# Softmax tiles turned by VectorE and a trip through DRAM in place of TensorE transposes

## The chip, the cores and the metric

The kernel runs on one core of one Trainium2 chip. A core has a matrix engine (TensorE, PE in the profile, with its weight loads shown as PEld), a vector engine (VectorE, DVE), an activation engine (ScalarE, ACT), a general engine (GpSimd, POOL) and a queue engine (SyncE, SP), all working in order, each on its own list of instructions; sixteen DMA engines move data between DRAM and the on-chip memory (SBUF). TensorE writes its results to PSUM, which the profile names ps with a tag. The metric is the device time of one execution in microseconds (us); lower is better.

## The reference

One layer of an encoder over 512 tokens of width 1024, all in float32:

- four token mixers fed by one input projection of h = RMSNorm(x): A, a differential attention with 4 heads (two softmaxes per head, subtracted, over chunks of 64 tokens); F, a forgetting attention with 8 heads of 64 (causal, with a bias from a cumulative sum); C, a convolution of width 31 with a LayerNorm; D, a short gated convolution. Each is projected to 1024, gated by sigmoids of h, summed, and projected again;
- a cross attention into 256 memory tokens;
- a gated MLP of width 2816 with a convolution of width 3.

The change lies in A and F. For a block of 128 queries:

```python
# A, per head: two softmaxes, subtracted, applied to v
p = softmax(where(mask, q @ k.T * scale, -inf))      # for c = 0 and 1
a = p[0] - lam * p[1]
o = a @ v
# F, per head
s = q @ k.T * scale + c_q - c_k
p = softmax(where(t_k <= t_q, s, -inf))
o = p @ v
```

## The kernel before

**Number format.** Products with float32 accuracy are made from three matmuls: each operand is split into a high part (a cast by ACT to the fp32r format) and a low part (the remainder, by DVE), and high x high, high x low and low x high are summed. Weights arrive in the raw tile `wr` by DMAs that SP issues (L175), ACT casts them to `wh` (L189), DVE makes `wl` (L190). There are four `wh` and four `wl` buffers, and weights are prepared three blocks ahead of the matmuls that use them. A block of the main work is 24 matmuls of 512 columns.

**Main work and background tasks.** The main line of the program is a sequence of such blocks (projections, gates, branch projections). The attentions are Python generators beside it, `a_task` (one per head) and `f_task` (one per pair of heads). An object `Background` counts a clock from the matmuls that the program has issued (`bg.clock`); a task's step ends with `yield cost, wait`, and it is taken up again when `wait` us of that clock have gone by and credit for `cost` is there. At most two tasks are open at a time, and `bg.drain` issues what is left of a task at once. Behind this, a planner orders the instructions of each engine by a priority from the program order and by its own estimate of when each becomes ready; on the chip each engine then follows its list in order.

**An attention task.** Queries come in four tiles of 128, keys up to the tile's end, so tile qt has (qt + 1) x 128 keys. In step s = 0 to 3 the scores of query tile s are made (PE, into PSUM tag `sc`), DVE takes the row maximum (L829 in A, L994 in F, where the bias tile `fbias`, made by POOL in L988 and L990, is added), ACT takes the exponential with its row sum (L834, L999), and DVE or ACT scales by the reciprocal (L838 and L839 in A, L1003 in F). The result lies in tile `e` as queries x keys. For the product with v it is needed as keys x queries. So in step s + 1, `to_keys_major` turns the tile of step s: TensorE transposes each 128 x 128 part into PSUM tag `tr` (L235), ACT casts it to `pth` (L154), and DVE makes `ptl` (L155). In steps 3 and 5 `values` multiplies two query tiles at a time: step 3 query tiles 0 and 1, step 5 query tiles 2 and 3. It issues matmuls of 256 columns, and of 128 for the last key tile. A's heads have three passes per key tile, F's two, since F's v holds its high and low part side by side in one stationary operand.

**Order and buffers around it.** A's four tasks run beside the last gate blocks of mixer C, F's four pairs beside those of mixer A. F's pair p + 1 does not pass its step 1 before pair p has finished. `e` has 3 buffers, `fbias` 2, `pth` and `ptl` 2 each; the PSUM tags `mm`, `av`, `sc` and `tr` have 2 banks each, and while the attentions run the main work uses only `mm`. After the last pair of F comes its own branch projection, whose matmuls need F's result `y`, with two gate blocks before them.

Of the kernel before, what the change touches and what calls it, by code (L numbers as in the profile page):

```python
# [16 lines left out]
F32 = mybir.dt.float32  # L17
F32R = mybir.dt.float32r
# [64 lines left out]
def hybrid_layer(ctx: ExitStack, tc: tile.TileContext, a: dict, out: bass.AP):  # L83
# [150 lines left out]
    def transpose(ps, x, n=P):  # L234
        PE.transpose(ps, x, ident[:n, :n])  # L235
        bg.clock += 0.107
# [544 lines left out]
        matmul(ps[:, :w], qk[:, c, q], qk[:, 2 + c, :w], True, False)  # L781
        matmul(ps[:, :w], qk[:, c, q], qk[:, 4 + c, :w], False, True)

    def to_keys_major(e, n, pt_h, pt_l, local):

        ps = bank("tr")
        for kt in range(n):
            transpose(ps[:, kt * P:(kt + 1) * P], e[:, kt * P:(kt + 1) * P])
        sl = slice(local * P, (local + 1) * P)
        split(ps[:, :n * P].rearrange("p (k c) -> p k c", k=n), pt_h[:, :n, sl], pt_l[:, :n, sl])  # L790

    def values(ps, terms, pt, half):


        n = 2 * half + 2
        for kt in range(n):
            q0 = P if kt == n - 1 else 0
            passes = terms(kt)
            for i, (v, p) in enumerate(passes):
                matmul(ps[:, half * 256 + q0:half * 256 + 256], v, pt[p][:, kt, q0:256],  # L800
                       kt == 0 and i == 0, kt == n - 1 and i == len(passes) - 1)

    def pt_tiles():
        return (m1p.tile([P, 4, 256], F32R, tag="pth", name="pth", bufs=2),
                m1p.tile([P, 4, 256], F32R, tag="ptl", name="ptl", bufs=2))


    def a_task(h, qk, v):
        es, pt, av = {}, None, None
        for step in range(6):  # L810
            if step in (3, 5):
                if av is None:
                    av = bank("av")
                vh, vl = (x[:, :, h * P:(h + 1) * P] for x in v[0])
                values(av, lambda kt: ((vh[:, kt], 0), (vh[:, kt], 1), (vl[:, kt], 0)), pt, step // 2 - 1)
            cost = 0.0
            if 1 <= step <= 4:
                if step in (1, 3):
                    pt = pt_tiles()
                to_keys_major(es.pop(step - 1)[:, 0], step, pt[0], pt[1], (step - 1) % 2)  # L820
                cost += 0.1 + 0.15 * step
            if step < 4:
                qt, w = step, (step + 1) * P
                e = es[qt] = e4()
                st = m1p.tile([P, 8], F32, tag="st8", name="st8", bufs=4)
                for c in range(2):
                    ps = bank("sc")
                    scores(ps, qk, c, qt * P, w)
                    V.tensor_tensor_reduce(e[:, c, :w], ps[:, :w], mask_a[:, S - w:], scale=1.0,  # L829
                                           scalar=-3.0e38, op0=ALU.add, op1=ALU.max,  # L830
                                           accum_out=st[:, c:c + 1])
                V.tensor_scalar(st[:, 2:4], st[:, 0:2], -HD ** -0.5, None, ALU.mult)
                for c in range(2):
                    A.activation(e[:, c, :w], e[:, c, :w], AF.Exp, bias=st[:, 2 + c:3 + c],  # L834
                                 scale=HD ** -0.5, accum_out=st[:, 4 + c:5 + c])
                V.reciprocal(st[:, 6:8], st[:, 4:6])
                V.tensor_scalar(st[:, 7:8], st[:, 7:8], lam, None, ALU.mult)
                A.activation(e[:, 1, :w], e[:, 1, :w], AF.Copy, scale=st[:, 7:8])  # L838
                V.scalar_tensor_tensor(e[:, 0, :w], e[:, 0, :w], st[:, 6:7], e[:, 1, :w], ALU.mult,  # L839
                                       ALU.subtract)  # L840
                cost += 0.6 + 0.0035 * w
            if step == 5:
                e = e4()
                A.copy(e[:, 0], av)
            yield cost, 3.5

        ps = bank("tr")
        for t in range(NT):
# [102 lines left out]
    def f_task(p, qk, v):  # L951
        f_steps[p] = 0
        while f_steps[p - 1] < 4:
            yield 0.0, 0.5
        ck = []
        for j in range(2):
            t = m1p.tile([P, S], F32, tag="ck", name="ck", bufs=2)
            G.dma_start(t, crows[2 * p + j:2 * p + j + 1, :].rearrange("a s -> (a s)").partition_broadcast(P))
            ck.append(t)
        yield 0.0, 2.0  # L960
        es, pts, av = {}, None, None
        for step in range(6):
            if step in (3, 5):
                if av is None:
                    av = [bank("av"), bank("av")]
                for j in range(2):
                    hl = v[0][:, :, 2 * p + j]
                    values(av[j], lambda kt: ((hl[:, kt], 0), (hl[:, kt], 1)), pts[j], step // 2 - 1)
            while step == 1 and f_steps[p - 1] < 6:
                yield 0.0, 0.5  # L970
            f_steps[p] = step + 1
            cost = 0.0
            if 1 <= step <= 4:
                if step in (1, 3):
                    pts = [pt_tiles() for _ in range(2)]
                e = es.pop(step - 1)
                for j in range(2):
                    to_keys_major(e[:, j], step, pts[j][0], pts[j][1], (step - 1) % 2)
                cost += 0.1 + 0.3 * step
            if step < 4:  # L980
                qt, w = step, (step + 1) * P
                e = es[qt] = e4()
                st = m1p.tile([P, 8], F32, tag="st8", name="st8", bufs=4)
                for j in range(2):
                    head = 2 * p + j
                    bias = m1p.tile([P, S], F32, tag="fbias", name="fbias", bufs=2)

                    G.tensor_scalar(bias[:, :w], ck[j][:, :w], -1.0, cq[:, qt, head:head + 1],  # L988
                                    ALU.mult, ALU.add)
                    G.affine_select(out=bias[:, w - P:w], in_=bias[:, w - P:w], pattern=[[-1, P]],  # L990
                                    compare_op=ALU.is_ge, fill=BIG, base=0, channel_multiplier=1)
                    ps = bank("sc")
                    scores(ps, qk, j, qt * P, w)
                    V.tensor_tensor_reduce(e[:, j, :w], ps[:, :w], bias[:, :w], scale=1.0,  # L994
                                           scalar=-3.0e38, op0=ALU.add, op1=ALU.max,
                                           accum_out=st[:, j:j + 1])
                V.tensor_scalar(st[:, 2:4], st[:, 0:2], -HD ** -0.5, None, ALU.mult)
                for j in range(2):
                    A.activation(e[:, j, :w], e[:, j, :w], AF.Exp, bias=st[:, 2 + j:3 + j],  # L999
                                 scale=HD ** -0.5, accum_out=st[:, 4 + j:5 + j])  # L1000
                V.reciprocal(st[:, 6:8], st[:, 4:6])
                for j in range(2):
                    V.tensor_scalar(e[:, j, :w], e[:, j, :w], st[:, 6 + j:7 + j], None, ALU.mult)  # L1003
                cost += 0.6 + 0.0038 * w
            yield cost, 4.5
        if "f" not in y:
            y["f"] = (y8(), y8())

        e = e4()
        for j in range(2):  # L1010
            A.copy(e[0:HD, j], av[j][HD:P])
            V.tensor_tensor(e[j * HD:(j + 1) * HD, 0], av[j][0:HD], e[0:HD, j], ALU.add)
        split(e[:, 0], y["f"][0][:, p], y["f"][1][:, p])
        yield 1.8, 0.0
# [717 lines left out]
```

## Time and profile before

| what | value |
|---|---|
| time, median of 3 runs | 1063.66 us (1062.95 to 1064.75) |
| time of the profiled execution | 1062.93 us |
| span of its instructions | 1060.7 us |
| TensorE busy | 1050.7 us, 5357 matmuls |
| DVE, ACT, POOL busy | 796.7, 497.1, 148.1 us |
| A's attention lies at about | 230 to 365 us of the span |
| F's attention lies at about | 390 to 530 us of the span |

How to read it: a line of a group is `line engine operation out<-in shapes xcount | busy us, mean ns of one | idle time of the engine before them, and what ended it`. A line in order of time begins with its start and its length in us; neighbours of one kind are merged (x4), and in brackets stands how long the engine had been idle and who released it. A matmul's own length is that of one instruction in a pipeline, so the distance between the starts of two tells more than the length of one. The profile does not count issuing a DMA as busy time. `ACTq`, `SPq` and `POOLq` are the engines' queues of such issues.

### The profile page before, as it was taken

To read this page: it belongs to the slowest core of one execution; us is meant where nothing else is said; L and a number is where in the kernel's file an instruction comes from. 1 tells how busy PE (TensorE), PEld (TensorE's weight loads), DVE (VectorE), ACT (ScalarE), POOL (GpSimd) and SP (SyncE) were. 2 spreads that over 40 slices of the span, in tenths; PEclk is the share of its full clock that TensorE was granted. 3 is DMA by queue.
4 is the path that set the end of the run, shared out by engine and by line. 5 is a ranking of instruction groups with operands and counts; after the bars stand their busy time and mean duration, and the time that the engine had idled before them with its cause. 6 is when DMAs were issued, how large, how long until landed. Compare 5 with 4: busy or idle time off the path is not lost.

```text
span 1060.7 us, 14540 instructions
## 1 busy us (share of the span) xinstructions
PE 1050.7 (99%) x5357; PEld 892.6 (84%) x5357; DVE 796.7 (75%) x1261; ACT 497.1 (47%) x817; POOL 148.1 (14%) x248
## 2 busy tenths in 40 slices
PE   9999999999999999999999999999999999999997
PEld 7888888888888988888888899999888888888885
DVE  6999997567666358766575888786778787777796
ACT  5322222367565256655443665664333333445662
POOL 4000000000001015322110031031111211111001
PEclk9999999999999999999999999999999999999999
DMA  8944333322222252332344744226566776725672
GB/s 278 300 144 104 107 93 99 96 84 80 78 81 62 54 147 88 94 98 81 120 140 144 267 144 119 81 80 198 179 224 213 237 228 211 236 80 179 206 220 80
DMA packets 162107, 152.57 MB, mean 144 GB/s; under 512 B 5567, under 2 KB 135212, under 8 KB 162037
## 3 DMA queue, kind: packets, MB, share of 16 engines
q1 hardware_dynamic: 153139, 120.04, 37.6%
q10 hardware_dynamic: 6338, 23.08, 5.8%
q0 software_dynamic: 2560, 8.54, 2.8%
q8 instruction: 42, 0.69, 0.3%
q14 instruction: 28, 0.23, 0.1%
HBM read 133.79 MB, written 17.84 MB: 143 GB/s over the span
## 4 chain that ended last, share of the span: by engine, by line
PE 94%; DMA 2%; DVE 2%; ACT 1%; issue 1%; SPq 0%; POOLq 0%; DVEq 0%; POOL 0%; ACTq 0%
PE ps_mm L231 51%; PE ps_av L231 29%; PE ps_sc L231 6%; PE ps_tr L235 3%; PE ps_tr L231 2%; DMA dw<-sums 2%; DVE wl L1534 1%; PE ps_mm L440 1%; DMA e<-in_w_in 1%; PE ps_av L440 1%; ACT wh L1533 0%; DVE o L1632 0%; DVE htl L1534 0%; DVE n L1534 0%; ACT n L1533 0%
## 5 line engine op out<-in xcount | busy, mean ns | idle before, releaser
L189 ACT CAST wh<-wr 128x1024 fp32r<-128x1024 f32 (+1 forms) x142 | 148.6, 1050 | 273.6 <-PE ps_mm L231 173.5
L190 DVE TENSOR_TENSOR wl<-wr,wh 128x1024 fp32r<-128x1024 f32 (+1 forms) x142 | 178.0, 1256 | 89.4 <-ACT wh L189 89.1
L231 PE MATMUL ps_mm<-hth,wh 128*128 128x512 f32 (+1 forms) x616 | 231.4, 382 | 0.3 <-ACT hth L154 0.2
L231 PE MATMUL ps_mm<-htl,wh 128*128 128x512 f32 (+1 forms) x616 | 230.1, 380 | 0.0
L231 PE MATMUL ps_mm<-hth,wl 128*128 128x512 f32 (+1 forms) x616 | 229.8, 379 | 0.0
L231 PEld LDWEIGHTS ps_mm<-hth,wh 128*128 128x128 f32 x616 | 114.1, 188 | 21.7 <-ACT hth L154 0.8
L231 PEld LDWEIGHTS ps_mm<-hth,wl 128*128 128x128 f32 x616 | 114.0, 188 | 21.0
L231 PEld LDWEIGHTS ps_mm<-htl,wh 128*128 128x128 f32 x616 | 114.1, 188 | 20.4
L231 PE MATMUL ps_av<-hth,wh 128*128 128x512 f32 (+1 forms) x328 | 122.6, 374 | 0.0
L231 PE MATMUL ps_av<-htl,wh 128*128 128x512 f32 (+1 forms) x328 | 122.5, 373 | 0.0
L231 PE MATMUL ps_av<-hth,wl 128*128 128x512 f32 (+1 forms) x328 | 122.4, 373 | 0.0
L662 DVE SCALAR_TENSOR_TENSOR y<-y,par,y 128x482 f32<-128x482 f32 (+29 forms) x120 | 83.6, 738 | 0.2
L231 PEld LDWEIGHTS ps_av<-hth,wl 128*128 128x128 f32 x328 | 61.6, 188 | 10.8
L231 PEld LDWEIGHTS ps_av<-hth,wh 128*128 128x128 f32 x328 | 61.6, 188 | 10.8
L231 PEld LDWEIGHTS ps_av<-htl,wh 128*128 128x128 f32 x328 | 61.6, 188 | 10.8
L1534 DVE TENSOR_TENSOR wl<-dw,wh 128x1024 fp32r<-128x1024 f32 x32 | 40.2, 1261 | 12.8 <-ACT wh L1533 12.6
L1533 ACT CAST wh<-dw 128x1024 fp32r<-128x1024 f32 x32 | 33.5, 1051 | 22.6 <-PE ps_tr L231 7.5
L988 POOL TENSOR_SCALAR fbias<-ck,cq 128x128 f32<-128x128 f32 (+3 forms) x32 | 27.5, 865 | 68.8 <-DVE st L994 63.5
L1482 ACT ACTIVATE th<-c 128x512 f32<-128x512 f32 x22 | 13.9, 631 | 48.6 <-DVE c L592 45.9
L154 ACT CAST pth<-ps_tr 128x512 fp32r<-128x512 f32 (+3 forms) x56 | 23.4, 448 | 22.1 <-PE ps_tr L235 21.9
L592 DVE SCALAR_TENSOR_TENSOR c<-ps_mm,par,c 128x510 f32<-128x510 f32 (+1 forms) x44 | 32.7, 744 | 0.7
L155 DVE TENSOR_TENSOR ptl<-ps_tr,pth 128x512 fp32r<-128x512 f32 (+3 forms) x56 | 28.0, 513 | 6.1 <-ACT pth L154 5.8
(468 smaller groups left out, 2098.8 us busy)
## 6 DMA issues: line engine op xcount, KB each, us to landing
wr<-in_w_up SPq DMA_DIRECT2D x44, 512.0 KB
wr<-in_w_in SPq DMA_DIRECT2D x38, 512.0 KB
wr<-in_w_gate SPq DMA_DIRECT2D x32, 512.0 KB
wp<-in_w_down ACTq DMA_DIRECT2D x22, 512.0 KB
sums<-wp ACTq DMA_DIRECT2D x22, 512.0 KB
dw<-sums SPq DMA_DIRECT2D x44, 256.0 KB
wr<-in_w_branch SPq DMA_DIRECT2D x16, 512.0 KB
wide<-in_w_out SPq DMA_DIRECT2D x12, 512.0 KB
```

The lines of the kernel that those rows point to most:

```text
L154: A.copy(hi, ps)
L155: V.tensor_tensor(lo, ps, hi.bitcast(F32), ALU.subtract)
L189: order(A.copy(hi, raw[:, :n]))
L190: low.tensor_tensor(lo, raw[:, :n], hi.bitcast(F32), ALU.subtract)
L231: PE.matmul(ps, lhs, rhs, start=start, stop=stop)
L235: PE.transpose(ps, x, ident[:n, :n])
L440: keep(PE.matmul(banks[c][:, :S // 2], w[p == 1][:, k, c * P:(c + 1) * P], ht[p == 2][:, i * 4 + k, :S // 2], start=(i, p, k) == (0, 0, 0) ...
L592: ins = V.scalar_tensor_tensor(dst[:, s:], src[:, :S - s], w(k), dst[:, s:], ALU.mult, ALU.add)
L662: ins = V.scalar_tensor_tensor(dst[:, s:], src[:, :S - s], pc("conv_dw", k * 4 + j), dst[:, s:], ALU.mult, ALU.add)
L988: G.tensor_scalar(bias[:, :w], ck[j][:, :w], -1.0, cq[:, qt, head:head + 1], ALU.mult, ALU.add)
L1533: A.copy(hi, x)
L1534: V.tensor_tensor(lo, x, hi.bitcast(F32), ALU.subtract)
```

## The change

The 128 x 128 transposes by TensorE in `to_keys_major` go. In their place:

- DVE turns the scaled tile in squares of 32 x 32 (`V.transpose`). Which keys share a square is chosen by reading with a stride: key 4j + b of a block of 128 goes to quarter b, place j (`by_quarters`). In A the turn itself reads with the stride of four elements; in F the exponential reads with it, so that the turn of F's two heads is contiguous and in place.
- `put` stores the turned tile in a DRAM tile `turned` (6 buffers), at the end of the same step, by a DMA that ACT issues. F stores both heads in one.
- In the next step `to_keys_major` loads it back with an access pattern that brings the squares to the partitions where they belong (ACT issues one load per head), straight into the place of the low part; ACT casts that to the high part and DVE subtracts in place.
- `values` reads its moving operand in pieces of 32 columns from the new layout of `pth` and `ptl`, with as many columns in all.
- F's maximum pass writes its sum back into `fbias` and no longer into `e`, and the exponential reads it there.
- The waits behind steps 2 and 4, ahead of the two `values`, are raised to 6.0 us (from 3.5 in A and 4.5 in F), and the steps' costs are a little higher. The clock of `Background` no longer counts the transposes.

```diff
-    def to_keys_major(e, n, pt_h, pt_l, local):
-        ps = bank("tr")
-        for kt in range(n):
-            transpose(ps[:, kt * P:(kt + 1) * P], e[:, kt * P:(kt + 1) * P])
-        sl = slice(local * P, (local + 1) * P)
-        split(ps[:, :n * P].rearrange("p (k c) -> p k c", k=n), pt_h[:, :n, sl], pt_l[:, :n, sl])
+    def by_quarters(x):
+        return x.rearrange("p (t j b) -> p b t j", b=4, j=32)
+
+    def put(e, w):
+        n = e.shape[1]
+        d = dram.tile([2, P * S], F32, tag="turned", name="turned", bufs=6)[:n, :P * w]
+        d = d.rearrange("h (p x) -> p h x", p=P)
+        A.dma_start(d, e[:, :, :w])
+        return d
+
+    def to_keys_major(d, n, pt_h, pt_l, local):
+        hi, lo = (pt[:, local, :, :n].rearrange("p a t i -> p a (t i)") for pt in (pt_h, pt_l))
+        raw = lo.bitcast(F32)
+        A.dma_start(raw, d.rearrange("(a j) (b x) -> (j b) a x", j=32, b=4))
+        A.copy(hi, raw)
+        V.tensor_tensor(lo, raw, hi.bitcast(F32), ALU.subtract)
...
     def values(ps, terms, pt, half):
-                matmul(ps[:, half * 256 + q0:half * 256 + 256], v, pt[p][:, kt, q0:256],
+                matmul(ps[:, half * 256 + l * P:half * 256 + 256].rearrange("p (a i) -> p a i", i=32), v,
+                       pt[p][:, l:, :, kt].rearrange("p l a i -> p (l a) i"),
...
     def pt_tiles():
-        return (m1p.tile([P, 4, 256], F32R, tag="pth", name="pth", bufs=2),
-                m1p.tile([P, 4, 256], F32R, tag="ptl", name="ptl", bufs=2))
+        return tuple(m1p.tile([P, 2, 4, 4, 32], F32R, tag=n, name=n, bufs=2) for n in ("pth", "ptl"))
...
     def a_task(h, qk, v):
                 V.scalar_tensor_tensor(e[:, 0, :w], e[:, 0, :w], st[:, 6:7], e[:, 1, :w], ALU.mult,
                                        ALU.subtract)
-                cost += 0.6 + 0.0035 * w
+                V.transpose(e[:, 1, :w].rearrange("p (b t j) -> p b t j", b=4, j=32), by_quarters(e[:, 0, :w]))
+                es[qt] = put(e[:, 1:], w)
+                cost += 0.6 + 0.0045 * w
...
-            yield cost, 3.5
+            yield cost, 6.0 if step in (2, 4) else 3.5
...
     def f_task(p, qk, v):
-                    V.tensor_tensor_reduce(e[:, j, :w], ps[:, :w], bias[:, :w], scale=1.0,
+                    V.tensor_tensor_reduce(bias[:, :w], ps[:, :w], bias[:, :w], scale=1.0,
...
-                    A.activation(e[:, j, :w], e[:, j, :w], AF.Exp, bias=st[:, 2 + j:3 + j],
+                    A.activation(e[:, j, :w].rearrange("p (b t j) -> p b t j", b=4, j=32), by_quarters(biases[j][:, :w]),
+                                 AF.Exp, bias=st[:, 2 + j:3 + j],
...
                 for j in range(2):
                     V.tensor_scalar(e[:, j, :w], e[:, j, :w], st[:, 6 + j:7 + j], None, ALU.mult)
-                cost += 0.6 + 0.0038 * w
-            yield cost, 4.5
+                    V.transpose(e[:, j, :w], e[:, j, :w])
+                es[qt] = put(e, w)
+                cost += 0.6 + 0.0058 * w
+            yield cost, 6.0 if step in (2, 4) else 4.5
```

More of the change, by code (lines that the diff above doesn't have):

```diff
@@ L796, in values @@
         for kt in range(n):
-            q0 = P if kt == n - 1 else 0
+            l = int(kt == n - 1)
             passes = terms(kt)
             for i, (v, p) in enumerate(passes):
-                matmul(ps[:, half * 256 + q0:half * 256 + 256], v, pt[p][:, kt, q0:256],
+                matmul(ps[:, half * 256 + l * P:half * 256 + 256].rearrange("p (a i) -> p a i", i=32), v,
+                       pt[p][:, l:, :, kt].rearrange("p l a i -> p (l a) i"),
                        kt == 0 and i == 0, kt == n - 1 and i == len(passes) - 1)
     def pt_tiles():
-        return (m1p.tile([P, 4, 256], F32R, tag="pth", name="pth", bufs=2),
-                m1p.tile([P, 4, 256], F32R, tag="ptl", name="ptl", bufs=2))
+        return tuple(m1p.tile([P, 2, 4, 4, 32], F32R, tag=n, name=n, bufs=2) for n in ("pth", "ptl"))
     def a_task(h, qk, v):
@@ L823, in a_task @@
                 qt, w = step, (step + 1) * P
-                e = es[qt] = e4()
+                e = e4()
                 st = m1p.tile([P, 8], F32, tag="st8", name="st8", bufs=4)
@@ L981, in f_task @@
                 qt, w = step, (step + 1) * P
-                e = es[qt] = e4()
+                e = e4()
                 st = m1p.tile([P, 8], F32, tag="st8", name="st8", bufs=4)
+                biases = []
                 for j in range(2):
@@ L986, in f_task @@
                     bias = m1p.tile([P, S], F32, tag="fbias", name="fbias", bufs=2)
+                    biases.append(bias)
                     G.tensor_scalar(bias[:, :w], ck[j][:, :w], -1.0, cq[:, qt, head:head + 1],
```

## The prediction

> **What bounds the kernel now.** I read the page first (busy shares, the chain that ended last), then the waits of TensorE, then the windows of the two attention stages, the groups by shape, and at last single instructions in order of time. Page, span and busy shares:
> ```profile
> span 1060.7 us, 14540 instructions
> PE 1050.7 (99%) x5357; PEld 892.6 (84%) x5357; DVE 796.7 (75%) x1261; ACT 497.1 (47%) x817; POOL 148.1 (14%) x248
> ```
> The chain that ended last, by line, and the waits of TensorE:
> ```profile
> by line: PE ps_mm L231 51.4%; PE ps_av L231 29.4%; PE ps_sc L231 6.0%; PE ps_tr L235 3.3%; PE ps_tr L231 2.3%; DMA dw<-sums 1.9%; issue 0.7%; DVE wl L1534 0.6%; PE ps_mm L440 0.6%; DMA e<-in_w_in 0.5%; PE ps_av L440 0.5%; ACT wh L1533 0.4%;
> PE ps_mm L384 <- DVE e L334: 1.3, 1, 1.3
> PE ps_tr L424 <- DVE nt L419: 1.2, 2, 1.0
> PE ps_mm L231 <- ACT hth L154: 0.2, 1, 0.2
> ```
> TensorE is busy 99% of the span and waits 2.7 us for other engines in all, none of it behind the attentions. The windows (columns: busy us and count of PE, PEld, DVE, ACT, POOL, then clock, DMA share, GB/s) of A's attention, of the forgetting attention F, and of both with what lies between:
> ```profile
> 236.00:366.00 130.00, 130.00 (x724) 112.80 (x723) 80.89 (x195) 71.13 (x148) 9.97 (x17) 1.00 0.24 70
> 400.00:530.00 130.00, 129.91 (x673) 110.10 (x672) 89.58 (x207) 69.89 (x149) 39.05 (x68) 1.00 0.32 98
> 236.00:530.00 294.00, 293.89 (x1577) 252.01 (x1576) 190.50 (x443) 160.56 (x327) 54.31 (x96) 1.00 0.30 89
> ```
> In both, TensorE has no hole, DVE is at 62 to 69%, ACT near 54%, DMA at a quarter to a third, the granted clock 1.00. So a piece of TensorE work that goes shortens the span by its own length, as long as what replaces it arrives in time: the question is only lateness.
>
> **What is removed from TensorE.** A turns 4 heads x (1+2+3+4) tiles, F 4 pairs x 2 heads x 10: 120 transposes. The 32 of A's result and the 4 of the forget rows stay. Group row, and one burst of four in order of time:
> ```profile
> L235 PE MATMUL ps_tr<-ident,e 128*128 128x128 f32 x152 | 23.2, 273 | 0.0
> 259.05 0.39 PE L231 MATMUL ps_mm<-htl,wh 128*128 128x512 f32 x1
> 259.28 0.60 PE L235 MATMUL ps_tr<-ident,e 128*128 128x128 f32 x4
> 259.63 0.48 PE L231 MATMUL ps_mm<-hth,wl 128*128 128x512 f32 x1
> 259.95 0.39 PE L231 MATMUL ps_mm<-hth,wh 128*128 128x512 f32 x1
> ```
> The 273 ns is a pipelined duration; the price is spacing. Matmuls of 512 columns follow each other every 0.23 us (259.05 to 259.28). From 259.28 to 259.95 lie four transposes and one matmul: 0.67 - 0.23 = 0.44, so 0.111 each. The chain agrees in size: 3.3% of 1060.7 is 35 us for all the transposes of L235, some 320. Term one: 120 x 0.111 = **13.3 us less**.
>
> The Trainium skill, VectorE: DVE Perf Modes, section Rules for kernel authors, says to turn a 128x128 tile on TensorE if PSUM is an acceptable destination, and its section The three transpose paths gives 390 ns for one in bf16; the rule speaks against the change. By 390 ns each the removed work would be 46.8 us and the time near 1018; by the spacing in this trace it is 13.3 us, and the trace decides.
>
> **What TensorE gets instead.** The 168 value matmuls (A 4 x 18, F 8 x 12) keep their column counts, but the moving operand is now read in pieces of 32 columns from blocks 128 apart, where it was one run of 256 or 128. No row shows such a read. A gain is excluded, since the columns are equal. At the other end is half the rate: 0.12 us more for each (their spacing, 509.65 to 509.77 in the rows further down), +20.2 us. I take 0, since each piece is still one run, like the rows.
>
> **What DVE gets.** 16 squares-of-32 transposes in A, 32 in F, over 128, 256, 384 and 512 columns (12 of each). No row shows one; the nearest is a pass over one such tile, here with the ACT rows that matter:
> ```profile
> L155 DVE TENSOR_TENSOR ptl<-ps_tr,pth 128x512 fp32r<-128x512 f32 x12 | 8.0, 685 | 3.6 <-ACT pth L154 3.6
> L155 DVE TENSOR_TENSOR ptl<-ps_tr,pth 128x384 fp32r<-128x384 f32 x12 | 6.4, 550 | 0.9 <-ACT pth L154 0.8
> L155 DVE TENSOR_TENSOR ptl<-ps_tr,pth 128x256 fp32r<-128x256 f32 x12 | 4.9, 420 | 1.0 <-ACT pth L154 0.8
> L155 DVE TENSOR_TENSOR ptl<-ps_tr,pth 128x128 fp32r<-128x128 f32 x12 | 3.2, 283 | 0.1
> L154 ACT CAST pth<-ps_tr 128x512 fp32r<-128x512 f32 x12 | 6.6, 586 | 10.4 <-PE ps_tr L235 10.4
> L154 ACT CAST y<-e 128x512 fp32r<-128x512 f32 x4 | 2.5, 622 | 3.3 <-DVE e L1012 3.3
> L189 ACT CAST wh<-wr 128x1024 fp32r<-128x1024 f32 x39 | 40.7, 1046 | 41.0 <-PE ps_mm L231 33.8 <-PE ps_av L231 4.3 <-DMA wr<-in_w_in 1.4
> ```
> 12 x (0.685 + 0.550 + 0.420 + 0.283) = 23.3 us; twice that, 46.5, if the turn or A's strided read of it runs at half rate; less than nothing is excluded, as no DVE work goes. DVE goes from 190.5 to 214 (at most 237) of 294 us, 73 to 81%: it stays off the path, 0 in the sum. The subtraction of L155 stays, from SBUF.
>
> **What ACT and the queues get.** Stores: 16 in A, 16 in F (both heads in one). Loads: 16 in A, 32 in F. All 80 are issued by ACT, at the 0.33 us that such an issue takes (first row; then F's exponentials, min/median/max in ns, and the one trip through DRAM in these stages, in order of time):
> ```profile
> 753.31 0.33 ACTq L547 DMA_DIRECT2D sums<-wp  x1
> L999 ACT ACTIVATE e<-e,st x32: 386/556/726, 397.1 to 511.3; 128x128 f32<-128x128 f32 x8, 128x256 f32<-128x256 f32 x8, 128x384 f32<-128x384 f32 x8, 128x512 f32<-128x512 f32 x8
> 387.86 0.57 POOL L941 DMA_DIRECT2D crows<-e  x1 [30.58 <-DVE e L940]
> 390.40 1.11 POOL L958 DMA_DIRECT2D ck<-crows  x2 [1.97 <-DMA crows<-e]
> 394.20 0.37 POOL L988 TENSOR_SCALAR fbias<-ck,cq 128x128 f32<-128x128 f32 x1 [2.69 <-DMA ck<-crows]
> 394.98 0.29 DVE L994 CUSTOM_DVE_ANT_0 e<-ps_sc,fbias 128x128 f32<-128x128 f32 x1 [2.63 <-POOL fbias L990]
> ```
> 80 x 0.33 = 26.4 us of issue; 48 casts from SBUF instead of PSUM at +0.036 (622 against 586 ns), 1.7 us; F's 32 exponentials now read with a stride, from 0 to once their 32 x 0.556 = 17.8 us more. ACT goes from 160.6 to 189 to 206 of 294 us, before waits. New waits stand on it: a store waits for DVE's turn, a load for the store to land, the cast for the load. Behind them in ACT's order are the weight casts of L189, the gate activations of L1029 and the exponentials; DVE's weight remainders wait for the casts, TensorE for those. The cover is in L189's row: of its 41 us of idle time 33.8 ended when TensorE freed a buffer, and with four weight buffers of each kind they run three blocks of 24 matmuls ahead, 3 x 24 x 0.23 = 16.6 us. While that holds, ACT's waits cost 0; if it goes, each us of wait is a us of span. SP's and POOL's queues get no instruction more; SP's weight loads share the DMA engines with 120 tiles of 64 KB stored and loaded, 15.7 MB, over 294 us 54 GB/s beside 89: 0, and if that slowed the loads, L189 would end its idle time on DMA.
>
> POOL: F's bias tile (2 buffers) is now held until the exponential, not until the maximum of L994:
> ```profile
> 503.39 2.32 POOL L988 TENSOR_SCALAR fbias<-ck,cq 128x512 f32<-128x512 f32 x2 [3.83 <-DVE st L994]
> 505.33 0.62 ACT L999 ACTIVATE e<-e,st 128x384 f32<-128x384 f32 x1
> ```
> The next bias could start at 505.95 instead of 503.39, 2.5 us later in a step. POOL is busy 39 of 130 us there, so this is chain length, not load; it counts at F's end.
>
> **The length of the new chain.** The last pair of F (scaled tile; transposes; ptl; first value matmul; result y; first matmul that needs y), and the first pair's first half, the tightest:
> ```profile
> 512.51 0.88 DVE L1003 TENSOR_SCALAR e<-e,st 128x512 f32<-128x512 f32 x2
> 519.04 1.04 PE L235 MATMUL ps_tr<-ident,e 128*128 128x128 f32 x8
> 520.29 1.29 DVE L155 TENSOR_TENSOR ptl<-ps_tr,pth 128x512 fp32r<-128x512 f32 x2 [1.25 <-ACT pth L154]
> 524.46 0.28 PE L231 MATMUL ps_av<-pth,v 128*128 128x256 f32 x1
> 528.93 0.69 DVE L155 TENSOR_TENSOR y<-e,y 128x512 fp32r<-128x512 f32 x1 [0.69 <-ACT y L154]
> 531.80 0.62 PE L231 MATMUL ps_av<-y,wh 128*128 128x512 f32 x2
> 404.23 0.59 DVE L1003 TENSOR_SCALAR e<-e,st 128x256 f32<-128x256 f32 x1
> 412.16 0.40 PE L231 MATMUL ps_av<-pth,v 128*128 128x256 f32 x2
> 509.65 0.28 PE L231 MATMUL ps_av<-pth,v 128*128 128x256 f32 x1
> 509.77 0.28 PE L231 MATMUL ps_av<-ptl,v 128*128 128x256 f32 x1
> ```
> A store's leg, from the crows rows, is 2.5 us (387.86 to 390.40). A load's is 3.8 (390.40 to 394.20), with two slower POOL issues in it. At 512 columns F then needs 1.4 (two turns) + 2.5 + 3.8 + 1.2 (casts) + 0.7 = 9.6 us from the scaled tile to the first value matmul; the rows leave 524.46 - 513.39 = 11.1. At 256 columns: 0.8 + 2.5 + 3.8 + 0.7 + 0.4 = 8.2 against 412.16 - 404.82 = 7.3. The raised yields (6.0 for 4.5 in F, for 3.5 in A) ask 1.5 to 2.5 us more room before the value matmuls, which covers the deficit. So TensorE doesn't wait inside the stages: 0. At F's end the chain must finish before the matmul at 531.80, ready at 529.62, a cover of 2.2 us. TensorE comes there earlier by the transposes of the last pair, 20 x 0.111 = 2.2 us, and the chain starts later by one raised yield, 1.5: 2.2 + 1.5 - 2.2 = **+1.5 us**. The ends: 0 if the planner uses the 5.6 us that the tile lay before it was turned (513.39 to 519.04); and, if it keeps that room and puts both legs on top, with POOL's delay, 2.5 + 3.8 + 2.5 + 2.2 - 2.2 = 8.8. I stay near the lower end, since that room is in the rows.
>
> **Sum.** The profiled execution took 1062.93 us, 0.7 below the median of 1063.66. 1062.93 - 13.3 + 1.5 = 1051.1; on the median 1051.9, so **1052 us**.
>
> **Rivals.**
> 1. *The end of F pays more*: 8.8 instead of 1.5: 1063.7 - 13.3 + 8.8 = 1059. For it: drained steps have no other work planned between them. Against: 11.1 us of room in the last rows. Chance 0.14.
> 2. *TensorE waits at the value matmuls* (slower). Orders are written by a planner ahead of time, and in the crows rows DVE stood 2.63 us for a trip through DRAM that came later than planned. There are 16 groups of value matmuls; TensorE takes them in order, so it waits with the main blocks behind. It decides from 13.3 / 16 = 0.83 us each; at 1.5 each, between that and the 2.63, 1063.7 - 13.3 + 24 = 1074. Against: the room above, DMA only 0.3 busy. Chance 0.14. The Trainium skill, DMA: Bandwidth & Descriptors, Specifications, puts line rate at 512 bytes and more, and the loads here move 128 to 512 bytes at a time, which would make this rival likelier; no run here shows it yet.
> 3. *ACT becomes the bound* (slower): in 32 steps ACT waits once for a store and once for a load. Wholly uncovered that is 32 x (2.5 + 3.8) = 202 us, and 189 + 202 = 391 us of ACT in the 294 of the stages, 1161. It decides where 189 + 64 waits make 294, at 1.64 us each; at 1.8, 1074, which I take. Against: two tasks interleave, and the planner can put other ACT work ahead of a wait. Chance 0.11.
> 4. *The broken-up reads cost double*: 1063.7 - 13.3 + 20.2 = 1071. Nothing in the trace speaks for it. Chance 0.06.
> 5. *Nothing is gained*, lateness eating just the 13.3: 1062 to 1066. Chance 0.05.
>
> **Numbers.** The forecast has 0.50 (its own range 1049 to 1056: all cover holds, to half the end's bound), rival 1 0.14. Faster 0.64, same 0.05, slower 0.31, with 0.2% (2.1 us) as what this kernel's runs (1062.95 to 1064.75) can tell from no change. The range starts at 1048, the case without any loss (1050.4) less what a measurement can't tell, and ends at 1073, with about half of rivals 2 and 3 above it, 0.13.
>
> **What would show it.** Right: 120 fewer L235 rows; TensorE without waits in both windows, which end 6 to 9 us sooner; value matmuls 0.12 apart. Wrong: waits of PE for ptl; L189 idle that ends on anything but TensorE; turns above 1.4 us at 512 columns; store or load legs above 4 us; the first y matmul waiting for y.

## The result, and the profile after

The kernel with the change takes **1090.16 us** (median of 4 runs, 1086.97 to 1093.96) against 1063.31 us for the kernel before on the same chip: a ratio of 1.0248, 95% interval 1.0228 to 1.0267. The forecast was 1052, the range 1048 to 1073. The direction was wrong, and the time lies 17 us above the range.

The page of the changed kernel (its profiled execution took 1086.97 us): span, busy shares, and the chain that ended last by engine.

```profile
span 1084.8 us, 14527 instructions
PE 1047.3 (97%) x5237; PEld 885.7 (82%) x5237; DVE 821.2 (76%) x1309; ACT 509.0 (47%) x817; POOL 140.1 (13%) x248
PE 82%; DMA 7%; DVE 5%; ACT 4%; issue 2%; ACTq 0%; POOL 0%; POOLq 0%; DVEq 0%; SPq 0%
```

The 120 transposes are gone (5237 matmuls for 5357), and yet the span is 24.1 us longer. ACT is no fuller than it was (47%), but the chain now runs through DMA for 7% of the span (2% before). The same two windows of the attentions as before the change (busy us and count of PE, PEld, DVE, ACT, POOL, then clock, DMA share, GB/s):

```profile
236.00:366.00 130.00, 125.67 (x669) 107.33 (x668) 90.89 (x207) 71.55 (x148) 9.54 (x17) 1.00 0.38 110
400.00:530.00 130.00, 119.88 (x565) 99.71 (x564) 97.37 (x230) 74.31 (x138) 33.07 (x72) 0.97 0.53 150
```

TensorE was full in both and now has 4.3 and 10.1 us of holes in them. What TensorE waited for between 225 and 565 us (us in total, times, longest), and the first three rows and the fifth of what ACT waited for there:

```profile
PE ps_mm L231 <- ACT ge L1048: 8.0, 1, 8.0
PE ps_mm L231 <- DVE qk L772: 7.3, 3, 3.4
PE ps_av L231 <- ACT pth L801: 5.5, 5, 3.4
PE ps_mm L231 <- DVE qk L763: 2.0, 1, 2.0
PE ps_mm L231 <- DVE v L155: 1.4, 1, 1.4
PE ps_sc L231 <- DVE st L844: 1.4, 1, 1.4
PE ps_sc L231 <- DVE qk L772: 0.8, 2, 0.6
PE ps_av L231 <- DVE ptl L802: 0.6, 1, 0.6
```
```profile
ACT pth L801 <- DMA ptl<-turned: 38.1, 25, 4.6
ACT e L1015 <- DVE st L1013: 21.1, 10, 4.1
ACT wh L189 <- PE ps_mm L231: 15.9, 11, 6.3
...
ACT e L1015 <- issue: 8.7, 1, 8.7
```

The first table sums to 27.0 us where there was nothing before. Only 6.1 us of it (the two `ps_av` rows) is TensorE waiting for the turned tiles. 18.7 us is the main work (`ps_mm`) waiting for a PSUM bank that ACT or DVE has not yet emptied: by the gate's tanh (L1048), by the casts and remainders of q and k (L762 to L772), by the split of v. The second table says why ACT is late: it stands 38.1 us at the cast for a load to land, and once 8.7 us at an issue.

Two POOL instructions just ahead of the largest hole, and then the chain that ended last between 526 and 545 us, in order of time (start, length, what):

```profile
527.82 0.58 POOL L1143 DMA_DIRECT2D g_mem<-in_norm_mem  x1
528.39 0.54 POOL L1177 DMA_DIRECT2D m_t<-in_mem  x1
```
```profile
528.75 6.83 DMA turned<-e
...
535.65 0.37 ACTq L800
...
537.78 1.37 ACT e L1015 x3
539.15 0.93 ACT wh L189
540.08 0.59 ACT ge L1048
540.68 0.04 issue
540.72 4.31 PE ps_mm L231 x11
```

After the store's 6.83 us come, all in ACT's queue, the issue of the load that waited for it, the exponentials, a weight cast, and only then the tanh that empties TensorE's bank. TensorE stood from 532.76 to 540.72. The store shared the DMA engines with 1 MB that POOL had begun to load for the next stage (`g_mem`, `m_t`).

And behind a long hole the clock is low. Three stretches (busy us of PE, PEld, DVE, ACT, POOL, clock, DMA share, GB/s):

```profile
451.00:459.00 8.00, 5.03 (x13) 4.01 (x14) 4.76 (x10) 4.74 (x8) 1.01 (x3) 0.57 0.90 258
537.00:544.00 7.00, 3.28 (x8) 2.61 (x9) 4.30 (x8) 4.48 (x8) 0.00 (x0) 0.51 0.22 58
550.00:558.00 8.00, 6.39 (x23) 5.56 (x24) 3.18 (x6) 3.37 (x6) 0.00 (x0) 0.57 0.31 99
```

As an estimate, TensorE's busy time in each stretch times the share of the clock that is missing: 5.03 x 0.43 + 3.28 x 0.49 + 6.39 x 0.43 = some 6.5 us lost to the clock.

### The profile page after: what moved, and what is told of

The parts are those of the page before. It is cut to its first block, busy times and chain, and to the rows that moved or that the text cites. A ratio compares the mean times of both kernels' runs of the same rounds, so it can differ in the third digit from the quotient of the medians.

```text
span 1084.8 us, 14527 instructions
## 1 busy us (share of the span) xinstructions
PE 1047.3 (97%) x5237; PEld 885.7 (82%) x5237; DVE 821.2 (76%) x1309; ACT 509.0 (47%) x817; POOL 140.1 (13%) x248
## 4 chain that ended last, share of the span: by engine, by line
PE 82%; DMA 7%; DVE 5%; ACT 4%; issue 2%; ACTq 0%; POOL 0%; POOLq 0%; DVEq 0%; SPq 0%
PE ps_mm L231 41%; PE ps_av L231 28%; PE ps_sc L231 6%; DMA ptl<-turned 5%; PE ps_tr L231 4%; DMA turned<-e 2%; PE ps_tr L235 2%; ACT wh L189 1%; DVE wl L190 1%; ACT e L1015 1%; PE ps_mm L440 1%; PE ps_av L440 1%; DVE e L853 1%; ACT e L846 0%; DVE e L1020 0%
## 5 line engine op out<-in xcount | busy, mean ns | idle before, releaser
L189 ACT CAST wh<-wr 128x1024 fp32r<-128x1024 f32 (+1 forms) x142 | 148.6, 1048 | 248.1 <-PE ps_mm L231 150.4
L1015 ACT ACTIVATE e<-fbias,st 128x128 f32<-128x128 f32 (+3 forms) x32 | 27.6, 865 | 31.6 <-DVE st L1013 21.1
L801 ACT CAST pth<-ptl 128x128 fp32r<-128x128 f32 (+3 forms) x48 | 21.6, 457 | 38.5 <-DMA ptl<-turned 38.1
L802 DVE TENSOR_TENSOR ptl<-ptl,pth 128x128 fp32r<-128x128 f32 (+3 forms) x48 | 23.6, 496 | 19.4 <-ACT pth L801 19.1
L231 PE MATMUL ps_mm<-y8b,wh 128*128 128x512 f32 x96 | 32.4, 415 | 6.0 <-DVE qk L772 3.9
```

The source lines that it names most:

```text
L189: order(A.copy(hi, raw[:, :n]))
L231: PE.matmul(ps, lhs, rhs, start=start, stop=stop)
L801: A.copy(hi, raw)
L802: V.tensor_tensor(lo, raw, hi.bitcast(F32), ALU.subtract)
L1015: A.activation(e[:, j, :w].rearrange("p (b t j) -> p b t j", b=4, j=32), by_quarters(biases[j][:, :w]), AF.Exp, bias=st[:, 2 + j:3 + j], s ...
```

## The experiments

The edits are to the changed kernel, unless another is named, and the code lines are shortened. The runs were made in batches on different chips, on which the kernel before took 1061.99 to 1064.12 us, so a difference of 2 us between two batches says little. Theories: **Q**, ACT's in-order queue holds what empties the banks; **D**, the trip through DRAM is too long, whoever issues it; **S**, the softmax's own chain (strided exponential, turn) became too long; **P**, the planner's raised costs; **M**, the collision with POOL's loads; **B**, the cover of two banks.

### Which attention loses: r3, r4

`r3`: F's functions as before the change, A's as after. `r4`: the reverse.

```
-    to_keys_major, values, pt_tiles, softmax of f_task (r3) / a_task (r4) as changed
+    the same functions as before the change, for that attention alone
```

> Only attention A's tiles go through DRAM; F's are turned by TensorE as before (40 transposes fewer than before, 80 more than after). In the changed kernel A's stretch has some 5 us of holes on TensorE and F's some 22. Theories Q and S both: 1062 to 1068 us. If the loss were one of the DMA's legs alone it would be in proportion to the stores, 8 of the 32 tiles' rows in a third of the bytes: 1069 to 1073.

> Only attention F's tiles go through DRAM; A's are turned by TensorE as before (80 transposes fewer than before). Theories Q and S: F's holes of some 22 us and the low clock behind them stay, less 8.9 us of transposes: 1077 to 1090 us. If A and F hurt each other through SyncE's and ScalarE's queues: under 1072.

Measured: r3 1065.99 us (ratio 1.0024, 1.0012 to 1.0036), r4 1085.93 (1.0211, 1.0193 to 1.0230). Both lie where Q and S had put them. F carries most of the loss, A a little. No sign that the two hurt each other: r3's loss of 2.9 and r4's of 22.8 together are 25.7 of the 27.

### Whose queue: r1, r2

```
 def put(e, w):                                             r1
-    A.dma_start(d, e[:, :, :w])
+    SP.dma_start(d, e[:, :, :w])
 def to_keys_major(...):
-    A.dma_start(raw, d.rearrange(...))
+    SP.dma_start(raw, d.rearrange(...))
```
```
 def put(e, w):                                             r2
+    SP.dma_start(d, e[:, :, :w])
+    for j in range(n): SP.dma_start(e[:, j, :w]..., d[:, j]...)    # back into the softmax tile
 def to_keys_major(e, ...):
+    raw = e[:, :n * P]...                                  # the cast reads it there
```

> The changed kernel with only the queue of the stores and loads moved from ScalarE to SyncE. Theory Q (ScalarE's in-order queue holds what frees the two PSUM banks of the main stream: it stands at the store's issue for the turn, at the load's issue for the store, at the cast for the load): the first two waits leave ScalarE, the third stays (38.1 us in 25 waits): 1066 to 1082 us, and the hole of 7.96 us before the gate's tanh is gone. Theory D (the trip through DRAM is late for TensorE, whoever issues it): 1086 to 1094, the holes stay. Theory S (the added work of the softmax itself: strided exponentials, turns, the bias held): 1083 to 1091.

> Stores and loads on SyncE, and each load right behind its store, back into the softmax tile, so that the cast one step later finds its data there. Theory Q: all three waits leave ScalarE: 1050 to 1062 us and less than 5 us of holes on TensorE. Theory D: 1075 to 1094, since the way from store to cast is no shorter, only the load starts sooner. Theory S: 1078 to 1090, with holes before evictions that wait for L1015, L1018 and L1021.

Measured: r1 1078.81 us, r2 1083.53. Taking the issues off ACT gains 11.4 us, as Q said; but the big hole is still there (6.45 us), and r2, which should have taken away ACT's last wait, gained less and misses the 1050 to 1062 that Q asked. The chain of r1 at that hole shows what stands in the issue's place, and its row of ACT's waits how much:

```profile
525.64 6.75 DMA turned<-e
...
532.46 2.51 DMA ptl<-turned
...
535.04 0.04 ACT pth L801
...
536.41 0.69 ACT ge L1048
```
```profile
ACT pth L801 <- DMA ptl<-turned: 48.2, 29, 5.6
```

ACT now waits at the cast for store and load together: 48.2 us where it was 38.1. In r2 it was 53.1: the load followed its store at once, but at this hole the store's 6.75 us and the load's 2.71 us stood there as before. A queue can be changed; the trip stays in front of the cast. That is D's half of the truth.

### The chain ahead of the trip, the plan, the collision: r5 to r8

```
-    A.activation(e[:, j, :w].rearrange(...), by_quarters(biases[j][:, :w]), AF.Exp, ...)        r5
+    A.activation(e[:, j, :w], biases[j][:, :w], AF.Exp, ...)       # and A's turn likewise
-    V.transpose(...)                                               # r6: r5, and no turn at all
-    yield cost, 6.0 if step in (2, 4) else 4.5     (3.5 in A; 0.0058 and 0.0045 per column)     r7
+    yield cost, 4.5                                (3.5 in A; 0.0038 and 0.0035)
+    if p == 3 and step == 4:                       # r8: POOL reads the last ptl before it
+        G.tensor_copy(t[:, :1], pts[1][1][:, 1, 0, 0, :1]...)      # issues g_mem and m_t
```

> The changed kernel with its broken-up reads made plain: F's exponential and A's turn read their row in order (this leaves out the spreading by quarters, so the rows that come back are in another order). It takes 9.9 us off F's exponentials (8 of each width, 120, 244, 373 and 495 ns each) and 8.6 us off A's turns. Theory S (the longer chain exponential, reciprocal, scale, turn inside a step holds VectorE and ScalarE before the evictions): the holes before qk L772 and L763 mostly go, 1064 to 1076 us. Theory Q or the memory loads' collision: 1081 to 1089, the holes stay.

> As r5, and the turns in squares of 32 left out too: the tiles go through DRAM as they are. Another 15 us of VectorE, of it some 0.3 to 0.7 us a tile between the scale and the store. Theory S: 1058 to 1072 us, below r5. If only the strided reads mattered: equal to r5 within 2 us. Theory Q: within 6 us of the changed kernel.

> The changed kernel with the planner's costs and due times of before (3.5 and 4.5, 0.0035 and 0.0038 per column). Theory P (the raised costs and due times push F's steps to the end of the stage, where they run in a bunch): 1066 to 1080 us. If the plan is not the cause, the load follows its store sooner and ScalarE stands longer: 1086 to 1100.

> The changed kernel, with POOL's loads of g_mem and m_t (1 MB) held back until the last tile's legs have landed, by one small copy on POOL that reads the last ptl. Theory M (the store at 528.75 shares the DMA engines with these loads and lands some 4 us late, ScalarE stands 8.67 us for it, and the gate's tanh behind it leaves TensorE's bank full): the hole of 7.96 us shrinks below 3, 1077 to 1083 us. If the hole has another cause it stays: 1085 to 1093.

Measured: r5 1080.17, r6 1074.10, r7 1084.91, r8 1083.03 us. Each median is lower than the changed kernel's (by 10.0, 16.1, 5.3 and 7.1), and none gains what its theory asked. r7's gain is not clear: the interval of its ratio to the kernel before, 1.0177 to 1.0243, overlaps the 1.0228 to 1.0267 of the changed kernel. M comes nearest: r8 is at the upper edge of its range. In its trace the store at the hole takes 2.45 us, not 6.83, and the hole shrinks from 7.96 to 4.19 us, though not below the 3 that was expected:

```profile
530.26 2.45 DMA turned<-e
```

S looked good after r6. As a cause of its own it falls with r12.

### More cover for the main work: r9 to r11

F's tiles no longer use the two PSUM banks `tr`. The main work gets them in F's stretch.

```
 def bank(tag=None):
-        tag = "av" if turn_of.shared and turn_of.n % 2 else "mm"
+        tag = turn_of.other if turn_of.shared and turn_of.n % 2 else "mm"
         yield from vf_jobs(vf)
+        yield share(True, "tr")
         yield from kv_blocks(0)
 ...
         yield then(lambda: bg.drain("f"))
+        yield share(False)
```

r10 adds the edit of r1, r11 those of r1 and r8.

> The changed kernel, with the two PSUM banks 'tr', which F's tiles no longer use, given to the main stream in F's stretch (its groups take 'mm' and 'tr' in turn, four banks in place of two). Theory B (what is lost is TensorE standing at a full bank while ScalarE and VectorE are held up by the tiles' chain): of F's holes those at ps_mm, 17.3 us (8.0 gate tanh, 7.3 L772, 2.0 L763), go, and the half clock behind the two longest, some 5 us: 1064 to 1075 us. If TensorE stood for the tiles' data itself, the holes move to ps_av and the time stays at 1083 to 1092.

> As r9, with stores and loads on SyncE as in r1 (1078.8). Theory B: with the longer cover the queue matters less than it did (11 us): 1056 to 1070 us, at or below r9. If queue and banks are two separate losses that add, 1055 to 1060; if SyncE's weight loads come late behind the tiles' waits, above r9.

> As r10, with POOL's loads of g_mem and m_t held back as in r8. If the collision of the last tiles' legs with them still counts with four banks: 2 to 7 us below r10. If four banks cover it: within 2 us of r10.

Measured: r9 1075.39 us, r10 1068.25, r11 1069.28. With four banks the waits of 8.0, 7.3 and 2.0 us at `ps_mm` are gone but for 0.5 at the tanh. Of the 16.8 us of waits that are left in r9, 10.5 are TensorE waiting for the tiles themselves (its two `ps_av` rows), where it was 6.1, so a part of the holes moved there:

```profile
PE ps_av L231 <- ACT pth L801: 9.0, 7, 6.5
PE ps_av L231 <- DVE ptl L802: 1.5, 2, 0.9
```

So B is right about the place, and r9 lies 0.4 us above its range. Queue and banks together gain 21.9 us (11.4 and 14.8 alone), and with both, the collision no longer shows (r11); r10 and r11 lie where B had put them.

### The trip alone: r12, and what remains with r13, r14

```
 def put(e, w):                                                     r12
-    A.dma_start(d, e[:, :, :w]); return d
+    return e
 def to_keys_major(d, ...):
-    A.dma_start(raw, d.rearrange("(a j) (b x) -> (j b) a x", j=32, b=4))
+    raw = d[:, :n * P].rearrange("p (a x) -> p a x", a=4)          # no store, no load
```

r13 is r10 with the plain reads of r5. r14 is r10 with F's last pair done as before the change (`own = p == 3`), on two banks from there.

> The changed kernel without the store and the load: the cast reads the turned tile where it lies, one step later (this leaves out the second half of the turn, the exchange of the squares). Exponentials and turns stay as they are. If the trip (issues, waits for landing, collisions) is the larger share: 1062 to 1072 us. If the longer chain of strided exponential and turn is: 1074 to 1082 us.

> r10 (1068.25) with the plain reads of r5 (the order of the rows is left out). If strided reads hurt only through the two banks, which r10 doubled: within 3 us of r10. If they still hurt at the end of F and at ps_sc: 1058 to 1064 us.

> r10 with F's last pair of heads (p = 3) done as before: TensorE's transposes, no trip, the main stream back on two banks from there on. r10's two largest holes, 3.15 and 4.76 us, and the half clock behind them lie at the last tiles of F. Theory E (the end of F pays the trip openly): 1057 to 1062 us, below the kernel before. If the holes only move to the next pair: 1065 to 1070.

Measured: **r12 1053.79 us** (ratio 0.9904, 0.9889 to 0.9920), r13 1063.90, r14 1065.95. r12 is below both expectations. Its busy shares, all of TensorE's waits between 225 and 565 us, and three rows of a value-matmul group in order of time:

```profile
PE 1039.4 (99%) x5237; PEld 880.4 (84%) x5237; DVE 818.2 (78%) x1309; ACT 509.6 (48%) x817; POOL 139.8 (13%) x248
```
```profile
PE ps_sc L231 <- ACT qk L771: 0.8, 1, 0.8
PE ps_sc L231 <- DVE st L1005: 0.3, 1, 0.3
PE ps_av L231 <- DVE ptl L797: 0.3, 1, 0.3
PE ps_mm L231 <- DVE qk L772: 0.2, 1, 0.2
```
```profile
285.81 0.28 PE L231 MATMUL ps_av<-ptl,v 128*128 128x256 f32 x1
285.93 0.40 PE L231 MATMUL ps_av<-pth,v 128*128 128x256 f32 x2
286.17 0.28 PE L231 MATMUL ps_av<-ptl,v 128*128 128x256 f32 x1
```

Strided exponentials, turns, the bias held longer, the raised due times are all still in r12, and TensorE has 1.6 us of waits and full clock. So with the trip gone all of these together cost at most those 1.6 us, and the trip costs this kernel 1090.16 - 1053.79 = **36.4 us**. The traces add up: the spans differ by 1084.8 - 1052.8 = 32.0 us, and the rows give 27.0 - 1.6 = 25.4 us of waits and 6.5 us of low clock, 31.9. That r5 and r6 gained 10 and 16 us shows that strided reads and turns do cost time while the trip is there. VectorE's instructions ahead of the hole that ends at 409.25, in the changed kernel, show how:

```profile
406.62 0.17 DVE L1018 RECIPROCAL st<-st 128x2 f32<-128x2 f32 x1 [2.44 <-ACT e L1015]
406.82 0.89 DVE L1020 TENSOR_SCALAR e<-e,st 128x256 f32<-128x256 f32 x2
407.63 0.75 DVE L1021 STREAM_TRANSPOSE e<-e 128x256 f32<-128x256 f32 x2
408.41 0.69 DVE L772 TENSOR_TENSOR qk<-ps_mm,qk 64x512 fp32r<-64x512 f32 x1
```

The remainder that empties the bank (L772) stands behind scale and turn, and these behind ACT's strided exponentials, which ACT began at 405.01, after it had issued two loads (403.48 to 404.63), the first of which had waited for a store that landed at 403.46. TensorE's waits behind L763 and L772 at `ps_mm` fall from 9.3 us to 5.9 in r5 and 2.2 in r6, while ACT's wait for loads at the cast does not fall (38.6 and 41.9 us, where it was 38.1). So I read it as one cover that is used up by the trip and the longer chain together; no run shows how it is shared out. With four banks and SyncE the plain reads are worth 4.4 us (r13, in the second of its ranges). r14 removed r10's two large holes (3.15 and 4.76 us), but only 2.3 us of time went: 20 transposes came back (2.2 us by the spacing), 7.5 us of small holes are left, and the low clock of one stretch. How these add up is open.

### Attempts at a faster kernel: r15 to r18

r15 issues the cast and the subtraction one pick-up of the task (a tick) after the load; r16 is r10 with that; r17 is r14 with that. r18 is r3 (A alone through DRAM) with stores and loads on SyncE.

```
-    A.copy(hi, raw); V.tensor_tensor(lo, raw, hi..., ALU.subtract)          r15, r16, r17
+    return parts                  # a closure with these two
-    yield cost, 6.0 if step in (2, 4) else 4.5
+    yield cost, 3.5               # 3.0 in A
+    for parts in todo: parts()
+    yield 0.0, 1.5
```

> The changed kernel with one thing moved: the cast and the subtraction of a loaded tile are issued a tick later than its load (due after 3.0 or 3.5, and 1.5 more to the next step) in place of right behind it. ScalarE's 38.1 us of waiting for the load to land at the cast should fall below 15; its waits at the issues stay. If the casts' waits are a main part of the trip's 36 us (1090.16 less r12's 1053.79): 1068 to 1080. If the issues' waits alone are: 1084 to 1092.

> r10 (four banks in F's stretch, both legs on SyncE; 1068.25) with the late casts of r15. All of ScalarE's waits for the trip but those at F's end are gone: 1058 to 1065 us, with the end of F as the largest holes. If the casts' waits were already covered by the four banks: 1066 to 1070.

> r16 with F's last pair turned by TensorE as in r14 (1065.95): no wait for the trip anywhere near the end. 1054 to 1060 us, below the kernel before, since r12 (1053.79) without the trip is its floor but for some 2.2 us of transposes. If what r14 lost against that floor is not a wait for the trip: 1062 to 1067.

> Only attention A's tiles through DRAM (r3, 1065.99), with its stores and loads on SyncE as in r1. r1's trace has some 2 us of holes on TensorE in A's stretch and the first F block where r3's has 5.07; 40 transposes fewer save 4.4 us. If waits on ScalarE are what A's part pays: 1060 to 1063 us, faster than the kernel before by up to 0.3%. If A's trip costs elsewhere: 1064 to 1067.

Measured: r15 1092.51, r16 1092.92, r17 1076.10 us, all misses, r16 24.7 us worse than r10. ACT's wait at the cast did not even fall (39.5 us in r15). F's last store starts at 552.60, where it started at 542.70 in the changed kernel, and its trip runs alone while TensorE stands 16.4 us in one piece for the cast behind it. I take it that the pick-up added to each step delays the tiles; that is not shown, as the waits of a task of F add up to 30 us in both. The last trip of F in r15 (DMA in the chain, in order of time):

```profile
552.60 2.74 DMA turned<-e
...
555.75 3.22 DMA ptl<-turned
```

These three therefore say nothing on which of ACT's waits counts.

**r18: 1061.28 us**, before 1063.14, ratio 0.9983 with interval 0.9970 to 0.9995. Of the versions that do all of the work it is the only one below both kernels, by 0.17%, which is less than the 0.2% that I had named as telling from no change, though the interval leaves 1 out. All of TensorE's waits between 225 and 565 us:

```profile
PE ps_mm L231 <- DVE v L155: 1.3, 1, 1.3
PE ps_sc L231 <- DVE st L868: 0.7, 1, 0.7
PE ps_mm L231 <- DVE ge L1079: 0.4, 1, 0.4
PE ps_sc L231 <- DVE qk L772: 0.2, 1, 0.2
```

40 transposes at 0.111 us are 4.4 us; less these 2.6 that is 1.8, and 1.9 was measured. SyncE instead of ACT is worth 4.7 us here (r3 to r18).

## Why the prediction was wrong

**Term one, 13.3 us less.** About right, some 2 us too high by r12: there TensorE was busy 1039.4 us for 1050.7, 11.3 less, and with 1.6 us of waits the time was 9.7 us below the kernel before on that chip (1053.79 for 1063.53).

**Value matmuls with a broken-up operand, 0.** Right: in r12 they are 0.12 us apart (285.81 to 285.93, and two from there to 286.17), as before.

**DVE's turns, 23.3 us, off the path.** The size is right: 8 times F's 280, 412, 553 and 696 ns and 4 times A's 407, 634, 866 and 1110 are 27.6 us, between the 23.3 and the 46.5. Off the path they are only without the trip. Group rows of the changed kernel by shape, for F's exponential, F's turn and A's turn at 512 columns and F's turn at 128:

```profile
L1015 ACT ACTIVATE e<-fbias,st 128x512 f32<-128x512 f32 x8 | 9.7, 1211 | 11.9 <-issue 8.7 <-DVE st L1013 3.3
L1021 DVE STREAM_TRANSPOSE e<-e 128x512 f32<-128x512 f32 x8 | 5.5, 696 | 0.0
L853 DVE STREAM_TRANSPOSE e<-e 128x512 f32<-128x512 f32 x4 | 4.4, 1110 | 0.1
L1021 DVE STREAM_TRANSPOSE e<-e 128x128 f32<-128x128 f32 x8 | 2.0, 280 | 0.0
```

F's turns cost what the nearest pass cost (696 and 280 ns against 685 and 283), A's strided ones at 512 columns 1.6 times that. The strided exponentials cost 9.9 us more in all, inside the 0 to 17.8. r12 shows that next to none of it is on the path when the trip is gone; r5, r6 and the rows of DVE above show that some of it is when the trip has used up the cover.

**"While that holds, ACT's waits cost 0."** This is the step that failed. The prediction named what is queued behind ACT's new waits: weight casts, gate activations, exponentials. Then it priced only the weight casts' cover, three blocks, 16.6 us. The gate activations and the casts of q and k have another: they empty the two `mm` banks. While one bank is being emptied TensorE fills the other, so the cover is one group, 24 x 0.23 = 5.5 us for a projection or gate, and half of that for a branch projection of 12. No row of TensorE's waits names a weight tile; 18.7 of their 27.0 us are at `ps_mm`. Doubling the banks took the three largest of these from the list (r9, 14.8 us of time), which shows it. 9.3 us of them come by way of DVE: its remainders of q and k (L763, L772) stand behind the scale and turn of a tile, and these behind ACT's exponentials.

**The legs, 2.5 and 3.8 us.** Right for a trip by itself: stores took 2.45 (r8) and 2.74 us (r15), loads 2.51 (r1) and 3.22. Wrong for a trip in company: 6.83 us beside POOL's 1 MB. Other company does it too. In r11, with POOL's loads held back, the last store started 0.6 us after a weight load of SyncE (525.15) and took

```profile
525.78 5.07 DMA turned<-e
```

The prediction asked only whether the tiles would slow the weight loads, not what else in the queues would slow the tiles. The list of signs had "legs above 4 us" on it, and that sign came.

**"TensorE doesn't wait inside the stages: 0."** The room was counted to the value matmuls, and there TensorE does wait only 6.1 us. 18.7 us were at a place that the sum did not look at.

**F's end, +1.5 (0 to 8.8).** Too small, inside its ends: without the trip F's end costs nothing (r12), with it the last hole is 3.45 us long, and the clock behind it costs 2.7 more (6.39 x 0.43). The hole of 7.96 us lies in the last pair too, but at a bank of the main work. In r14, doing the last pair the old way brings 2.3 us.

**POOL, the held bias.** Right that it is no load: DVE waited once for a bias, 0.8 us.

**The raised due times cover the deficit.** No run shows that they do: with the old ones (r7) the median is 5.3 us lower, with overlapping intervals. They don't move F's end: its last load is issued at 548.0 us in r7 and at 548.3 in the changed kernel.

**The rivals.** Rival 3 had the right engine and the right waits (store, then load), and the wrong test: it let ACT's waits count only once they filled ACT, at 64 times 1.64 us, 105 us. ACT waited some 52 us for the trip (38.1, 8.7, and 5.3 in two more waits for a store) and stayed at 47% busy; that was enough to be late for a bank 5.5 us deep. Rival 2 had the right sign and came true for 6.1 us. Its weight of 0.14 and rival 3's of 0.11 were too small together: both looked for one place where the trip must be covered, and there were three. And no step of the sum had the low clock around a hole, some 6.5 us.

## What to carry to other kernels

When a wait goes onto an in-order engine, list every instruction behind it by what it sets free, and price the wait against the shortest of these covers, not the longest: here the PSUM banks (5.5 us), not the weights (16.6 us). An engine that is half idle can still cost the path its full lateness. To price a trip, take it out alone and leave the rest (r12): shortening the work beside it (r5, r6) gains time too, because both draw on one cover, and looks like a cause of its own. And look at what a change frees: here two PSUM banks brought back 14.8 us of the 26.9 that the changed kernel had lost.

## What the runs showed of the hardware

Around three of the four holes over 3 us TensorE's granted clock was 0.50 for 6.8 us each (the windows above). It fell inside the hole: in the one from 450.81 to 453.97 at about 451.8, 1.0 us after its start. Around the fourth, 405.84 to 409.25, it stayed at 1.00 in every microsecond. The Trainium skill, TensorE: Matmul & The Clock Gate, Part 1, has a free-running activity window of about 3.4 us and half the clock after an idle one. The traces agree with the length of the window, as each low stretch here is two of them. They don't agree that a whole window must be idle: the hole that ended at 453.97 is 3.16 us long, and in r9 the clock was 0.50 from 270 to 276 us though no hole just before it was longer than 1.41 us. For holes of 3.16, 3.45 and 7.96 us the added loss in the changed kernel is much the same, some 2.2, 2.7 and 1.6 us.

Reading fp32 with a stride of four elements made an exponential of 512 columns 1211 ns instead of 715 (r5, where the same read is plain) and A's turn 1110 instead of 708; at 128 columns 514 instead of 395 and 407 instead of 310.

A store of 384 KB took 2.45 us by itself (r8) and 6.75 to 6.83 us beside 1 MB of loads from POOL's queue, whether ACT (the changed kernel) or SyncE (r1, r2) had issued it.
